# A GELU queued behind the next group's copy between PSUM banks

## The chip, the cores and the metric

The kernel runs on one core of one Trainium2 chip. The metric is the device time of one execution in microseconds (us). Below, TensorE is also PE (its weight loads PEld), VectorE is DVE, ScalarE is ACT, GpSimd is POOL and SyncE is SP, as the profile names them.

## What is computed

The program is a trunk of two decoder layers over 512 tokens of width 1024, in float32. Each layer has a mixer (attention and a short convolution in layer 0, gated linear attention in layer 1), then a gated MLP, then a per-layer embedding. The change touches the MLP alone:

```python
def _conv_ffn(h, w_up, conv_w, conv_b, w_down):
    u = _causal_depthwise_conv(h @ w_up, conv_w) + conv_b   # width 3, per column
    gate, up = jnp.split(u, 2, axis=-1)                     # 2816 columns each
    return (jax.nn.gelu(gate, approximate=False) * up) @ w_down
```

## The kernel before

Activations lie transposed: 128 features on the partitions, 512 tokens along the free dimension. Every float32 matmul is done as three passes over operands split into a high and a low part (`wh`, `wl` of weights, `uh`, `ul` of activations): ScalarE makes the high part by a copy, VectorE the low part by a subtraction (`split`, L109 and L110; `cut`, L142 and L143; `cut_blocks`, L819 and L820).

The up-projection (`ffn`) works through 11 column groups, `d` from 0 to 10. A group is 256 value columns and 256 gate columns. The value columns are two plain products (`value`, L162 to L164, 512 tokens wide), into the PSUM banks `V0` and `ps`. The gate columns use a scheme with seven half-size products instead of eight (`seven`, L872 to L874, 256 tokens wide), into the banks `W`, `V`, `X` and `Y`. Some products are summed on top of others, so the generator `seven` moves partial sums between banks by ScalarE copies, each of half a bank: L883 and L884 (W to X and Y), L890 (V to `more`), L893 (Y to X, here called the second copy) and L897 (X to Y). TensorE needs the second copy before it can go on with X's right half. To cover the copies, `seven` yields, and the loop puts pieces of the value product between: twelve matmuls 512 wide lie between the last product into Y's left half and the first product into X's right half.

While a group's products run, the weights of the next group are loaded (`loaded`, L941, one load of 1 MB for the value and one for the gate columns), cut and combined (L843, L844, L851, L854). The results of a group go through `taps`: scaling by the norm's row `R` (L923, L926, L929), then the three taps of the convolution, one on ScalarE (L930) and two on VectorE (L932). Two buffers tagged `zt` hold a group's gate half `g` and value half `y`; there are two of them, so the next group's L930 waits until they are read. Then come the GELU (L1061, ScalarE, 1024 wide), the product with the value half (`place`, L973 for the first four groups, L983 after that, VectorE), and in groups 4 to 9 `split_one(d - 4)`, which splits one of the activations kept by the first four groups (L109 and L110) for the down-projection. `split_acts` does the last two of these eight splits in the last group.

TensorE's instructions are issued in the order of the program text (`manual_schedule(engines={ET.PE})`). The other engines' orders are made when the program is built, by a scheduler that takes instructions by priority, which falls along the program text, as its own model of time finds them ready. On the chip each engine then takes its instructions in that fixed order and waits on semaphores. In the program before, the scheduler puts the GELU of group `d` behind the second copy of group `d + 1` for `d` from 0 to 4 and ahead of it for `d` from 5 to 9, and it pulls all eight splits into the time of groups 1 to 5.

Of the kernel before, what the change touches and what calls it, by code (L numbers as in the profile page):

```python
# [13 lines left out]
AF = mybir.ActivationFunctionType  # L14
# [42 lines left out]
class Kernel:  # L57
# [799 lines left out]
    def seven(self, od, ws, xg, forms, keep=True):  # L857

        nc = self.nc
        H = S // 2
        mm = nc.tensor.matmul
        W, V = self.pa(), self.pa()[:, :H]
        X, Y = self.ps(), self.ps()
        plain, t13, t2 = ws

        def product(out, w, c, x, first=False):
            kw = dict(skip_group_check=True)
            for j in range(ND // 2):  # L870
                (wh, wl), (xh, xl) = w(j, c), x(j)
                mm(out, wh, xh, start=first and j == 0, stop=False, **kw)  # L872
                mm(out, wh, xl, start=False, stop=False, **kw)  # L873
                mm(out, wl, xh, start=False, stop=j == ND // 2 - 1, **kw)  # L874

        def tokens(u, half):
            c = slice(half * H, (half + 1) * H)
            return lambda j: (xg[2 * j + u][0][:, c], xg[2 * j + u][1][:, c])

        s1, s2, s3, s4 = (lambda j, q=q: forms[j][q] for q in range(4))  # L880
        left, right = slice(0, H), slice(H, S)
        product(W[:, left], plain, 0, tokens(0, 0), True)
        nc.scalar.copy(X[:, left], W[:, left])  # L883
        nc.scalar.copy(Y[:, left], W[:, left])  # L884
        yield
        product(V, t13, 0, s1, True)
        more = V
        if keep:
            more = self.sp.tile([P, S], F32, tag="acc", name=self.nm("more"), bufs=1)[:, :H]
            nc.scalar.copy(more, V)  # L890
        product(X[:, left], plain, 1, tokens(1, 0))
        product(Y[:, left], t2, 0, s2)
        nc.scalar.copy(X[:, right], Y[:, left])  # L893
        yield
        last = self.cut_blocks(od)
        product(X[:, right], t13, 1, s3)
        nc.scalar.copy(Y[:, right], X[:, right])  # L897
        yield
        product(Y[:, left], last, 1, s4)
        product(X[:, right], last, 0, tokens(1, 1))  # L900
        yield X, Y, more

    def ffn(self, i, project, next_gain):


        nc, a, tc = self.nc, self.a, self.tc
# [5 lines left out]
        with tc.tile_pool(name=f"ffn{i}", bufs=1) as fp:  # L912
            self.mlp = fp
            kept, acts, fours = [None] * NF, [None] * NF, []
            groups = NF // 2

            def both():
                return fp.tile([P, 2, S], F32, tag="zt", name=self.nm("zt"), bufs=2)

            def taps(y, ps, f, more=None):  # L920
                z = fp.tile([P, S], F32, tag="z", name=self.nm("z"), bufs=3)
                if more is None:
                    nc.vector.tensor_tensor(z, ps, R, ALU.mult)  # L923
                else:
                    h2 = lambda x: x.rearrange("p (u t) -> p u t", u=2)
                    nc.vector.tensor_tensor(  # L926
                        h2(z), h2(ps), more.unsqueeze(1).to_broadcast([P, 2, S // 2]), ALU.add
                    )
                    nc.vector.tensor_tensor(z, z, R, ALU.mult)  # L929
                nc.scalar.activation(y, z, AF.Identity, scale=w2[:, f : f + 1], bias=bb[:, f : f + 1])  # L930
                for tap, w in ((1, w1), (2, w0)):
                    nc.vector.scalar_tensor_tensor(  # L932
                        out=y[:, tap:], in0=z[:, : S - tap], scalar=w[:, f : f + 1], in1=y[:, tap:],
                        op0=ALU.mult, op1=ALU.add,
                    )
# [11 lines left out]
            def value(w, ps, k0, k1):  # L947
                for k in range(k0, k1):
                    self.mm3(ps, w(k, 0, P), xg[k], start=k == 0, stop=k == ND - 1)

            def prepare(d):

                rv, rg = loaded(d)
                w1 = column(rv, 1)
                ev, od = self.by_parity(rg)
                ws = self.seven_forms(ev, od, rg)
                return self.seven(od, ws, xg, self.forms), w1, column(rv, 0)

            def begin(d, steps, w):

                ps = self.pa()
                value(w, ps, 0, 6)
                next(steps)
                value(w, ps, 6, ND)
                return lambda y: taps(y[:, 1], ps, NF + 2 * d + 1)

            def place(d, g, y):

                f = 2 * d
                if f < 8:  # L970
                    kept[f : f + 2] = [self.fp.tile([P, S], F32, tag=other[0], name=self.nm("u")) for _ in range(2)]
                    for u in range(2):
                        nc.vector.tensor_tensor(kept[f + u], g[:, u], y[:, u], ALU.mult)  # L973
                    return
                if d == groups - 1:
                    x = y
                else:
                    if f % 4 == 0:
                        fours.append(self.four(fp, F32))
                    x = fours[-1][:, f % 4 : f % 4 + 2]  # L980
                kept[f : f + 2] = [x[:, 0], x[:, 1]]
                pairs[f] = x
                nc.vector.tensor_tensor(x, g, y, ALU.mult)  # L983
# [3 lines left out]
            def split_one(f):  # L987

                tag = other[1 if f < 4 else 0]
                h = self.fp.tile([P, S], F32R, tag=tag, name=self.nm("uh"))  # L990
                pool, tag = (self.fp, tag) if f < 7 else (self.sp, "R")
                acts[f] = h, pool.tile([P, S], F32R, tag=tag, name=self.nm("ul"))
                self.split(acts[f], kept[f])
# [6 lines left out]
            def split_acts():  # L1000
                for f in (6, 7):
                    split_one(f)
# [32 lines left out]
            steps, w1c, w0c = ready  # L1035
            with tc.manual_schedule(engines={ET.PE}):
                late = begin(0, steps, w1c)
                for d in range(groups):
                    g, y = both(), both()
                    next(steps)  # L1040
                    V0 = self.pa()
                    value(w0c, V0, 0, ND // 2)
                    if d == 0:
                        self.end_norm()
                    next(steps)
                    value(w0c, V0, ND // 2, ND)
                    if d == 0:
                        R = self.spread()
                    X, Y, more = next(steps)
                    rest = late  # L1050

                    if d + 1 < groups:
                        steps, w1c, w0c = prepare(d + 1)
                        late = begin(d + 1, steps, w1c)
                    else:
                        split_acts()
                    rest(y)
                    taps(y[:, 0], V0, NF + 2 * d)
                    taps(g[:, 0], X, 2 * d)
                    taps(g[:, 1], Y, 2 * d + 1, more)  # L1060
                    nc.scalar.activation(g, g, AF.Gelu)  # L1061
                    place(d, g, y)
                    if 4 <= d < groups - 1:
                        split_one(d - 4)
            self.begin_norm(mine)
            finish = lambda m: self.advance(m, next_gain)
            if i == 1:
# [903 lines left out]
```

## Time and profile before

| | us |
|---|---|
| time before, median of 3 runs | 1207.76 |
| lowest and highest | 1206.56, 1208.12 |
| time of the profiled execution | 1206.43 |
| its span | 1204.7 |
| busy: PE, DVE, ACT | 1197.7, 968.3, 665.3 |
| granted TensorE clock, mean | 1.00 |
| GELUs (L1061), 22 | 23.4 busy, 1062 ns each |
| second copies and their like in the down-projections (L893), 29 | 365 ns each (median) |

The profile is of one execution. A row of a timeline gives the start and the duration in us, the engine, the line, the operation, what it writes and reads, and in brackets how long the engine sat idle before it and what ended that. A row of a stretch gives its bounds, its length, and the busy time of PE, PEld, DVE, ACT and POOL with the number of instructions, then the granted clock, the share of the DMA engines and GB/s. Ends of matmuls are modelled; their starts are recorded.

### The profile page before, as it was taken

To read this page: it belongs to the slowest core of one execution; us is meant where nothing else is said; L and a number is where in the kernel's file an instruction comes from. 1 tells how busy PE (TensorE), PEld (TensorE's weight loads), DVE (VectorE), ACT (ScalarE), POOL (GpSimd) and SP (SyncE) were. 2 spreads that over 40 slices of the span, in tenths; PEclk is the share of its full clock that TensorE was granted. 3 is DMA by queue.
4 is the path that set the end of the run, shared out by engine and by line. 5 is a ranking of instruction groups with operands and counts; after the bars stand their busy time and mean duration, and the time that the engine had idled before them with its cause. 6 is when DMAs were issued, how large, how long until landed. Compare 5 with 4: busy or idle time off the path is not lost.

```text
span 1204.7 us, 17692 instructions
## 1 busy us (share of the span) xinstructions
PE 1197.7 (99%) x7013; PEld 1036.9 (86%) x7013; DVE 968.3 (80%) x1527; ACT 665.3 (55%) x1081; POOL 43.8 (4%) x64
## 2 busy tenths in 40 slices
PE   9999999999999999999999999999999999999998
PEld 8877788999899889888988988889998899888887
DVE  6786587899998986746579876677999999988595
ACT  7466455656555644534573564555565645646374
POOL 2600000000000000000100000000000000000000
PEclk9999999999999999999999999999999999999999
DMA  7321322423333242222322222313242423322501
GB/s 222 93 85 45 96 74 70 140 71 108 103 106 104 91 137 97 96 89 94 115 93 68 73 70 71 105 49 127 70 141 70 136 75 120 134 88 97 210 1 70
DMA packets 111127, 117.61 MB, mean 98 GB/s; under 512 B 2840, under 2 KB 106322, under 8 KB 111044
## 3 DMA queue, kind: packets, MB, share of 16 engines
q1 hardware_dynamic: 109680, 115.35, 29.2%
q8 instruction: 55, 0.90, 0.3%
q0 software_dynamic: 560, 0.42, 0.3%
q10 hardware_dynamic: 804, 0.70, 0.2%
q14 instruction: 28, 0.23, 0.1%
HBM read 114.37 MB, written 2.10 MB: 97 GB/s over the span
## 4 chain that ended last, share of the span: by engine, by line
PE 87%; DVE 8%; ACT 2%; issue 1%; POOL 1%; DMA 0%; ACTq 0%; DVEq 0%; POOLq 0%
PE ps L162 12%; PE ps L163 12%; PE ps L164 12%; PE pa L163 7%; PE pa L162 7%; PE pa L164 7%; PE ps L872 5%; PE ps L874 5%; PE ps L873 5%; PE pa L872 2%; PE pa L874 2%; PE pa L873 2%; DVE wl L143 2%; PE ps L1371 1%; PE ps L1369 1%
## 5 line engine op out<-in xcount | busy, mean ns | idle before, releaser
L142 ACT ACTIVATE wh<-raw 128x1024 fp32r<-128x1024 f32 (+4 forms) x154 | 152.4, 991 | 155.1 <-PE ps L163 109.4
L143 DVE TENSOR_TENSOR wl<-raw,wh 128x1024 fp32r<-128x1024 f32 (+4 forms) x154 | 175.6, 1142 | 50.1 <-ACT wh L142 49.7
L819 ACT ACTIVATE wh<-raw 128x1024 fp32r<-128x1024 f32 x78 | 82.8, 1061 | 118.4 <-DVE raw L844 65.2
L932 DVE SCALAR_TENSOR_TENSOR zt<-z,vfa,zt 128x510 f32<-128x510 f32 (+1 forms) x176 | 130.6, 744 | 11.7 <-ACT zt L930 11.2
L820 DVE TENSOR_TENSOR wl<-raw,wh 128x1024 fp32r<-128x1024 f32 x78 | 95.3, 1222 | 19.3 <-ACT wh L819 19.2
L930 ACT ACTIVATE zt<-z,vfb 128x512 f32<-128x512 f32 x88 | 71.1, 810 | 28.9 <-DVE four L983 12.8
L162 PE MATMUL ps<-b,wh 128*128 128x512 f32 x192 | 76.8, 400 | 0.0
L163 PE MATMUL ps<-b,wh 128*128 128x512 f32 x192 | 75.1, 391 | 0.0
L164 PE MATMUL ps<-b,wl 128*128 128x512 f32 x192 | 75.0, 391 | 0.0
L163 PE MATMUL pa<-b,wh 128*128 128x512 f32 x176 | 69.0, 392 | 0.0
L163 PE MATMUL pa<-a,wh 128*128 128x512 f32 x176 | 69.0, 392 | 0.0
L162 PE MATMUL pa<-a,wh 128*128 128x512 f32 x176 | 69.0, 392 | 0.0
L162 PE MATMUL pa<-b,wh 128*128 128x512 f32 x176 | 69.0, 392 | 0.0
L164 PE MATMUL pa<-a,wl 128*128 128x512 f32 x176 | 68.4, 389 | 0.0
L164 PE MATMUL pa<-b,wl 128*128 128x512 f32 x176 | 68.4, 389 | 0.0
L872 PE MATMUL ps<-four,wh 128*128 128x256 f32 x232 | 65.1, 281 | 0.5 <-ACT ps L893 0.5
L874 PE MATMUL ps<-four,wl 128*128 128x256 f32 x232 | 64.4, 278 | 0.0
L873 PE MATMUL ps<-four,wh 128*128 128x256 f32 x232 | 64.2, 277 | 0.0
L162 PE MATMUL ps<-a,wh 128*128 128x512 f32 x160 | 63.1, 394 | 0.0
L163 PE MATMUL ps<-a,wh 128*128 128x512 f32 x160 | 62.6, 392 | 0.0
L164 PE MATMUL ps<-a,wl 128*128 128x512 f32 x160 | 62.5, 391 | 0.0
L162 PE MATMUL ps<-uh,wh 128*128 128x512 f32 x128 | 50.3, 393 | 0.0
(475 smaller groups left out, 3491.5 us busy)
## 6 DMA issues: line engine op xcount, KB each, us to landing
raw<-in_ffn_w_up_dram SPq DMA_DIRECT2D x44, 1024.0 KB, 5.0
raw<-in_ffn_w_down_dram SPq DMA_DIRECT2D x13, 1024.0 KB, 4.8
raw<-in_hy_w_in_dram SPq DMA_DIRECT2D x8, 1024.0 KB, 5.1
raw<-in_gla_w_in_dram SPq DMA_DIRECT2D x8, 1024.0 KB, 5.1
raw<-in_ffn_w_down_dram SPq DMA_DIRECT2D x8, 768.0 KB, 4.1
raw<-in_ple_w_gate_dram SPq DMA_DIRECT2D x6, 1024.0 KB, 4.8
raw<-in_hy_w_out_dram SPq DMA_DIRECT2D x16, 256.0 KB, 4.2
raw<-in_gla_w_out_dram SPq DMA_DIRECT2D x4, 1024.0 KB, 4.8
```

The lines of the kernel that those rows point to most:

```text
L142: nc.scalar.activation(hv, v, AF.Copy)
L143: nc.vector.tensor_tensor(lv, v, hv.bitcast(F32), ALU.subtract)
L162: mm(out, lh, rh, start=start, stop=False, **kw)
L163: mm(out, lh, rl, start=False, stop=False, **kw)
L164: mm(out, ll, rh, start=False, stop=stop, **kw)
L819: nc.scalar.activation(h, src, AF.Copy)
L820: nc.vector.tensor_tensor(l, src, h.bitcast(F32), ALU.subtract)
L872: mm(out, wh, xh, start=first and j == 0, stop=False, **kw)
L873: mm(out, wh, xl, start=False, stop=False, **kw)
L874: mm(out, wl, xh, start=False, stop=j == ND // 2 - 1, **kw)
L930: nc.scalar.activation(y, z, AF.Identity, scale=w2[:, f : f + 1], bias=bb[:, f : f + 1])
L932: nc.vector.scalar_tensor_tensor(out=y[:, tap:], in0=z[:, : S - tap], scalar=w[:, f : f + 1], in1=y[:, tap:], op0=ALU.mult, op1=ALU.add,)
```

## The change

`seven` keeps the instruction of the second copy in `self.copied`. In the loop, the GELU, `place` and `split_one` of a group become a function `ended`. It is called in the next turn of the loop, after the step of the generator that issues the second copy, inside `issue_after(self.copied.ins)`. That adds, for each instruction of the block on the copy's engine, which is ScalarE, an ordering edge behind the copy. So the GELU and the `uh` part of `split_one` (ScalarE) stand behind the next group's second copy in ScalarE's queue; `place` and the `ul` part (VectorE) follow them by their data and by their later place in the text. The first `next(steps)` moves ahead of `both()` in the loop. The last group's `ended` is called behind the loop, with no such edge.

```diff
         product(Y[:, left], t2, 0, s2)
-        nc.scalar.copy(X[:, right], Y[:, left])
+        self.copied = nc.scalar.copy(X[:, right], Y[:, left])
         yield
...
                 late = begin(0, steps, w1c)
+                ended = None
                 for d in range(groups):
+                    next(steps)
+                    if ended:
+                        with tc.issue_after(self.copied.ins):
+                            ended()
                     g, y = both(), both()
-                    next(steps)
                     V0 = self.pa()
                     value(w0c, V0, 0, ND // 2)
...
                     taps(g[:, 1], Y, 2 * d + 1, more)
-                    nc.scalar.activation(g, g, AF.Gelu)
-                    place(d, g, y)
-                    if 4 <= d < groups - 1:
-                        split_one(d - 4)
+
+                    def ended(d=d, g=g, y=y):
+                        nc.scalar.activation(g, g, AF.Gelu)
+                        place(d, g, y)
+                        if 4 <= d < groups - 1:
+                            split_one(d - 4)
+
+                ended()
```

## The prediction

> **What bounds the kernel now.** I read the page first, then the busy time of each engine in the stretches of the MLP up-projection, then the timelines around the copy that the change names. On the page TensorE (PE) is busy nearly the whole span.
>
> ```profile
> span 1204.7 us, 17692 instructions
> ...
> PE 1197.7 (99%) x7013; PEld 1036.9 (86%) x7013; DVE 968.3 (80%) x1527; ACT 665.3 (55%) x1081; POOL 43.8 (4%) x64
> ```
>
> That 99% is an average and its ends are modelled, so I looked at single column groups. The stretches below each run from the first value matmul behind one group's second copy to the same matmul of the next group (length first, then busy time of PE, PEld, DVE, ACT, POOL). The first five are of layer 0, the last three of layer 1.
>
> ```profile
> 213.66:234.25 20.59, 20.59 (x135) 18.63 (x133) 18.12 (x26) 12.50 (x17) 0.00 (x0) 1.00 0.32 102
> 275.42:296.01 20.59, 20.59 (x135) 18.63 (x133) 20.54 (x30) 12.03 (x20) 0.00 (x0) 1.00 0.31 103
> 296.01:316.94 20.93, 20.93 (x134) 18.65 (x133) 18.87 (x25) 12.12 (x18) 0.00 (x0) 1.00 0.30 101
> 316.94:338.06 21.12, 20.88 (x134) 18.58 (x133) 19.64 (x27) 11.95 (x17) 0.00 (x0) 1.00 0.32 101
> 379.24:399.82 20.58, 20.58 (x134) 18.62 (x133) 18.72 (x25) 11.33 (x16) 0.00 (x0) 1.00 0.31 103
> 895.29:915.88 20.59, 20.59 (x134) 18.63 (x133) 20.54 (x30) 11.90 (x20) 0.00 (x0) 1.00 0.32 103
> 915.88:936.72 20.84, 20.84 (x134) 18.66 (x133) 18.86 (x25) 12.10 (x18) 0.00 (x0) 1.00 0.31 101
> 936.72:957.82 21.10, 20.84 (x134) 18.53 (x133) 19.63 (x27) 11.91 (x17) 0.00 (x0) 1.00 0.31 101
> ```
>
> An undisturbed group takes 20.59 us, and it does so with VectorE (DVE) busy for 18.12, 18.72 or 20.54 of them. A period that does not follow VectorE's load is TensorE's own pace. Two groups in each layer are longer, and only those can be won. The Trainium skill (Perfetto Trace Analysis, Identifying the Most-Contended Engine) would judge TensorE by its weight loads, and 86% of them would leave room of some 168 us. The trace does not bear that out here: the loads are busy 18.63 us in every undisturbed group, whatever the other engines do.
>
> What makes the two groups longer is seen at the copy.
>
> ```profile
> 316.83 0.28 PE L874 MATMUL ps<-four,sq 128*128 128x256 f32 x1
> ...
> 319.46 0.39 PE L164 MATMUL pa<-a,wl 128*128 128x512 f32 x1
> 320.09 0.38 PE L872 MATMUL ps<-four,wh 128*128 128x256 f32 x1 [0.24 <-ACT ps L893]
> ...
> 316.56 1.06 ACT L819 ACTIVATE wh<-raw 128x1024 fp32r<-128x1024 f32 x1
> 318.70 1.06 ACT L1061 ACTIVATE zt<-zt 128x1024 f32<-128x1024 f32 x1 [1.08 <-DVE zt L932]
> 319.67 0.36 ACT L893 COPY ps<-ps 128x256 f32<-128x256 f32 x1
> ```
>
> The last product into Y's left half starts its last matmul at 316.83, so the copy could run when ScalarE (ACT) is done with L819, at about 317.6. But the GELU of the group before stands ahead of it, and waits 1.08 us for VectorE. The copy starts at 319.67, about 2.1 us late. TensorE has twelve value matmuls to cover that, then stands until 320.09. VectorE was late because of work that the scheduler had placed one group earlier: four splits of kept activations (L110) between 279 and 285 us, the reason for the 20.54 above.
>
> ```profile
> 279.42 1.28 DVE L110 TENSOR_TENSOR ul<-u,uh 128x512 fp32r<-128x512 f32 x2
> 281.29 0.68 DVE L110 TENSOR_TENSOR ul<-u,uh 128x512 fp32r<-128x512 f32 x1
> 284.29 0.68 DVE L110 TENSOR_TENSOR ul<-u,uh 128x512 fp32r<-128x512 f32 x1
> ```
>
> **The change, part by part.** Nothing is computed more or less: the built programs have the same instructions. In them TensorE's, SyncE's and GpSimd's orders are the same; only ScalarE's and VectorE's differ, inside the two up-projections.
>
> *The copy goes ahead of the GELU.* For five GELUs in each layer (those of groups 5 to 9) this is a swap; for groups 0 to 4 the copy was ahead already. The gain is what the two long groups hold over 20.59: (20.93 - 20.59) + (21.12 - 20.59) = 0.87 us in layer 0, and (20.84 - 20.59) + (21.10 - 20.59) = 0.76 us in layer 1, together 1.63 us. The later four swaps of a layer win nothing, since their groups take 20.59 already. The first long group, 20.93, has its copy ahead of the GELU even now; its excess should go because the cluster of splits goes (next part).
>
> *The GELU, the product behind it and the moved split wait for the copy.* What that costs is read from an undisturbed group with the old order.
>
> ```profile
> 399.71 0.28 PE L874 MATMUL ps<-four,sq 128*128 128x256 f32 x1
> 402.57 0.28 PE L872 MATMUL ps<-four,wh 128*128 128x256 f32 x1
> ...
> 398.61 1.06 ACT L819 ACTIVATE wh<-raw 128x1024 fp32r<-128x1024 f32 x1 [0.42 <-PE ps L873]
> 400.23 1.06 ACT L1061 ACTIVATE zt<-zt 128x1024 f32<-128x1024 f32 x1 [0.56 <-DVE zt L932]
> 401.19 0.37 ACT L893 COPY ps<-ps 128x256 f32<-128x256 f32 x1
> 402.58 0.82 ACT L930 ACTIVATE zt<-z,vfb 128x512 f32<-128x512 f32 x1 [1.02 <-DVE four L983]
> ...
> 401.32 1.23 DVE L983 TENSOR_TENSOR four<-zt,zt 128x1024 f32<-128x1024 f32 x1
> 403.43 1.54 DVE L932 SCALAR_TENSOR_TENSOR zt<-z,vfa,zt 128x511 f32<-128x511 f32 x2 [0.89 <-ACT zt L930]
> 405.13 1.23 DVE L143 TENSOR_TENSOR wl<-raw,wh 128x1024 fp32r<-128x1024 f32 x1 [0.16 <-ACT wh L142]
> 406.89 0.69 DVE L923 TENSOR_TENSOR z<-pa,R 128x512 f32<-128x512 f32 x1 [0.54 <-PE pa L164]
> 407.76 1.23 DVE L143 TENSOR_TENSOR wl<-raw,wh 128x1024 fp32r<-128x1024 f32 x1 [0.18 <-ACT wh L142]
> ```
>
> The copy becomes ready at 399.71 + 0.28 = 399.99 and can fill most of the 0.56 us in which ScalarE idles before the GELU. It would be out of the way by about 400.34 (0.37, less some overlap), so the GELU starts about 0.11 us later than at 400.23. What waits for that is the product L983, then L930 and L932 of the next group. Behind these VectorE idles 0.16 + 0.54 + 0.18 = 0.88 us, two of the three for work that TensorE releases. So 0.11 is absorbed, and I cost it at nothing. Without that cover it would cost 0.11 x 10 = 1.1 us, and if each GELU lost a whole copy, 0.37 x 10 = 3.7 us.
>
> *The splits (L109 on ScalarE, L110 on VectorE) move with it.* Six of a layer's eight now stand one by one behind the GELUs of groups 4 to 9, and the other two follow behind the last of these. Two L110 took 1.28 us above, so one adds some 0.6 us to VectorE in each of these groups, while groups 0 to 4 lose theirs. Its place is straight behind L983, where VectorE idles 0.89 us until L930 is done; 0.6 fits. On ScalarE the copy into `uh` fits into the 1.02 us before L930, which waits for L983 anyway. Behind the last group three splits stand together: 3 x 0.6 + 0.11 = 1.91 us against idle time of 0.89 + 0.88 = 1.77 us, so VectorE could be 0.14 us late there, 0.28 us over both layers. I take nothing for it, because it meets a weight cut for the down-projection and not a matmul, and keep 0.28 as the bound. Groups 1 to 4 only get lighter, and were at 20.59 already: no gain there.
>
> The sum is -1.63 us. The profiled execution took 1206.43 us (span 1204.7), so it would become 1204.8; the median of the runs is 1207.76, 1.33 above the profiled one, and becomes **1206.1 us**. A difference under 0.2% (2.4 us) is about what a measurement of this kernel can tell from no change, so this is a gain too small to be told for certain.
>
> **The rivals.**
>
> *More is won than the two groups.* The copies of this scheme have waiters of their own:
>
> ```profile
> L897 ACT COPY ps<-ps x29: 359/367/371, 197.8 to 1104.8; 128x256 f32<-128x256 f32 x29
> ...
>   PEld ps L872: 2.8, 8
> ```
>
> If the lighter VectorE queue also freed L897's eight waits, which lie partly in the down-projections, 2.8 us more would go: 1206.1 - 2.8 = 1203.3. For it: the cluster of splits delays whatever comes behind. Against it: the down-projections' order is unchanged.
>
> *Nothing is won.* The copy L893 goes early, but VectorE's lag lets another copy be late in the same group, and TensorE stands there instead: 1207.8. For it: the group of 20.93 us was long with its copy already ahead of the GELU. Against it: the cluster that made VectorE lag is itself gone.
>
> *The queue binds.* The GELU waits behind a copy that waits for TensorE, and the loop copy, GELU, L983, L930, L932 sets the pace. The price is the 1.1 to 3.7 us from above less 1.63: 1207.2 to 1209.8. It decides where the GELU slips by more than the 0.88 us of idle time; the rows make it 0.11. The Trainium skill (Perfetto Trace Analysis, Tensor Engine Instruction) says that ScalarE and VectorE are strict FIFOs, which is the rule against this change; the trace agrees in the rows at 318.70 and 319.67, where a ready copy stood behind a waiting GELU.
>
> *Slower: a weight cut holds the copy L897.* Without the splits the scheduler puts the cut L142 ahead of L897 in two more groups of each layer (1 and 3). L142 needs a load that has just landed. One group has this order already:
>
> ```profile
> 259.69 1.05 ACT L142 ACTIVATE wh<-raw 128x1024 fp32r<-128x1024 f32 x1
> 260.64 0.36 ACT L897 COPY ps<-ps 128x256 f32<-128x256 f32 x1
> ...
> 261.71 0.28 PE L872 MATMUL ps<-four,wh 128*128 128x256 f32 x1
> ...
> raw<-in_ffn_w_up_dram SPq DMA_DIRECT2D x44, 1024.0 KB, 5.0
> ```
>
> Here L897 ends at 261.00, 0.71 us before TensorE needs it. If ScalarE reaches the cut 2 us before its load (these take 5.0 us), TensorE stands 2.0 - 0.71 = 1.3 us in two groups of two layers, 5.2 us; less 1.63 that is +3.6: 1211.3. It decides from a load that is 0.71 us late. Against it: this group lost nothing, and the copy does not wait here.
>
> **How the numbers follow.** Forecast 0.54; more is won 0.15; nothing is won 0.13; the queue binds 0.07; a cut holds the copy 0.11. The forecast lies 0.8 us inside the 2.4 us line and the three runs spread over 1.6 us, so 0.04 of its 0.54 counts as faster. Faster: 0.15 + 0.04 = 0.19. Within 0.2%: 0.50 + 0.13 + 0.07 = 0.70. Slower: 0.11. The range goes from 1203.5, near the far end of the second case, to 1209.8, the upper price of the binding queue; it leaves out the slower case and some of the scatter.
>
> **What would show it.** Right: all ten stretches of each layer at 20.59 us; L893 ahead of L1061 everywhere and starting within 0.1 us of its last matmul or of L819's end; no waiter at L893; L110 one by one behind L983, with L932's idle of 0.89 shrunk to about 0.3. Wrong: a stretch over 20.7 us after the change; waits of TensorE on L897 or L883 in the up-projections; ScalarE's L142 waiting for a load ahead of L897; or GELUs that start later than 0.3 us behind VectorE's last L932.

## The result, and the profile after

The changed kernel takes 1205.18 us (median of 22 runs, 1204.47 to 1206.30) against 1207.15 us of the kernel before (22 runs, 1206.05 to 1208.16): 1.97 us less, a ratio of 0.9985 with a 95% interval of 0.9978 to 0.9991. That is a small gain, most of whose interval lies within the 0.2% that the prediction named. The profiled execution took 1205.84 us.

In the kernel after, lines up to 1030 keep their numbers, the GELU is L1067 and the residual add of the down-projection is L1189 (before: L1061 and L1181). The head of its page:

```profile
span 1204.1 us, 17688 instructions
...
PE 1196.2 (99%) x7013; PEld 1036.6 (86%) x7013; DVE 969.2 (80%) x1527; ACT 667.2 (55%) x1081; POOL 43.9 (4%) x64
```

Next the same stretches as in the prediction: from the first value matmul behind one group's second copy to that of the next group. Length, then busy time of PE, PEld, DVE, ACT, POOL. The first three are of layer 0, the last two of layer 1.

```profile
297.00:317.59 20.59, 20.59 (x134) 18.62 (x133) 19.50 (x26) 11.95 (x17) 0.00 (x0) 1.00 0.33 104
317.59:338.18 20.59, 20.59 (x135) 18.63 (x133) 19.33 (x26) 11.85 (x17) 0.00 (x0) 1.00 0.31 103
...
379.35:399.94 20.59, 20.59 (x135) 18.63 (x133) 19.34 (x26) 11.85 (x17) 0.00 (x0) 1.00 0.32 104
916.06:936.64 20.58, 20.58 (x134) 18.62 (x133) 19.65 (x27) 11.94 (x17) 0.00 (x0) 1.00 0.32 104
936.64:957.23 20.59, 20.59 (x135) 18.63 (x133) 19.34 (x26) 11.86 (x17) 0.00 (x0) 1.00 0.31 103
```

The four long stretches (20.93, 21.12, 20.84, 21.10) are gone. From the start of group 0's stretch to that of the last group's it is now 399.94 - 193.18 = 206.76 us in layer 0; before it was 399.82 - 192.18 = 207.64. In layer 1 it is 1018.99 - 812.23 = 206.76, before 1019.58 - 812.05 = 207.53. These are 0.88 and 0.77, the two terms of the sum. The spans differ by only 0.6, because in this one execution the work ahead of layer 0's groups took 1.0 us longer (193.18 against 192.18; in the traces of all kernels here it takes 192.0 to 193.6). ScalarE at the place where the copy had come 2.1 us late:

```profile
317.79 0.36 ACT L893 COPY ps<-ps 128x256 f32<-128x256 f32 x1 [0.35 <-PE ps L874]
318.06 1.06 ACT L1067 ACTIVATE zt<-zt 128x1024 f32<-128x1024 f32 x1
```

The copy now waits for TensorE and not for VectorE, and the GELU behind it waits for nothing. Of the 11 executions of `e4_down_pinned` below, one took 2004.04 us at a granted clock of 0.556; it is in the median but not in the ratio.

### The profile page after: what moved, and what is told of

It reads as the page before. It is cut to its first block, busy times and chain, and to the rows that moved or that the text cites. A ratio compares the mean times of both kernels' runs of the same rounds, so it can differ in the third digit from the quotient of the medians.

```text
span 1204.1 us, 17688 instructions
## 1 busy us (share of the span) xinstructions
PE 1196.2 (99%) x7013; PEld 1036.6 (86%) x7013; DVE 969.2 (80%) x1527; ACT 667.2 (55%) x1081; POOL 43.9 (4%) x64
## 4 chain that ended last, share of the span: by engine, by line
PE 88%; DVE 6%; issue 2%; ACT 2%; POOL 1%; DMA 0%; DVEq 0%; POOLq 0%; ACTq 0%
PE ps L162 12%; PE ps L163 12%; PE ps L164 12%; PE pa L163 7%; PE pa L162 7%; PE pa L164 7%; PE ps L872 6%; PE ps L874 6%; PE ps L873 5%; PE pa L872 2%; PE pa L874 2%; PE pa L873 2%; DVE wl L143 1%; PE ps L1379 1%; PE ps L1377 1%
## 5 line engine op out<-in xcount | busy, mean ns | idle before, releaser
L142 ACT ACTIVATE wh<-raw 128x1024 fp32r<-128x1024 f32 (+4 forms) x154 | 152.5, 992 | 156.8 <-PE ps L163 109.2
L143 DVE TENSOR_TENSOR wl<-raw,wh 128x1024 fp32r<-128x1024 f32 (+4 forms) x154 | 175.6, 1141 | 51.1 <-ACT wh L142 50.1
L819 ACT ACTIVATE wh<-raw 128x1024 fp32r<-128x1024 f32 x78 | 82.8, 1062 | 120.8 <-DVE raw L844 65.1
L932 DVE SCALAR_TENSOR_TENSOR zt<-z,vfa,zt 128x510 f32<-128x510 f32 (+1 forms) x176 | 130.7, 745 | 5.3 <-ACT zt L930 4.7
L930 ACT ACTIVATE zt<-z,vfb 128x512 f32<-128x512 f32 x88 | 71.1, 810 | 20.8 <-DVE four L983 8.3
L164 PE MATMUL ps<-b,wl 128*128 128x512 f32 x192 | 75.0, 391 | 0.0
L164 PE MATMUL pa<-a,wl 128*128 128x512 f32 x176 | 68.4, 389 | 0.0
L164 PE MATMUL pa<-b,wl 128*128 128x512 f32 x176 | 68.4, 389 | 0.0
L872 PE MATMUL ps<-four,wh 128*128 128x256 f32 x232 | 64.7, 279 | 0.0
L873 PE MATMUL ps<-four,wh 128*128 128x256 f32 x232 | 64.2, 277 | 0.0
L164 PE MATMUL ps<-a,wl 128*128 128x512 f32 x160 | 62.5, 391 | 0.0
```

Of the source, the lines that this page charges most:

```text
L142: nc.scalar.activation(hv, v, AF.Copy)
L143: nc.vector.tensor_tensor(lv, v, hv.bitcast(F32), ALU.subtract)
L164: mm(out, ll, rh, start=False, stop=stop, **kw)
L819: nc.scalar.activation(h, src, AF.Copy)
L932: nc.vector.scalar_tensor_tensor(out=y[:, tap:], in0=z[:, : S - tap], scalar=w[:, f : f + 1], in1=y[:, tap:], op0=ALU.mult, op1=ALU.add,)
```

## The experiments

A word on reading them: the medians of these kernels lie within 2 us of each other, at about the edge of what timing tells apart, but the undisturbed stretches of one trace repeat to 0.01 us, and group 0's stretch is 21.48 in every trace. So the verdicts rest on the stretches. Each trace is of one execution, though, and in layer 0 of two of them the work already starts later in group 0 than in all others; that is said there. Each label is the name of a kernel. A ratio in brackets is to the kernel before, with its interval.

**The two halves of the change, each alone.** First the order of GELU and copy without moving the splits (`e1_copy_first`):

```
                     with tc.issue_after(self.copied.ins): ended()    # ended(): GELU, place
...
+                    if 4 <= d < groups - 1: split_one(d - 4)         # at its old place in the text
```

> The order alone: the copy L893 goes ahead of the GELU as in the changed kernel, while the eight splits of a layer (L109, L110) keep their early, clustered places in groups 1 to 5. Cluster theory (VectorE's lag from the clustered splits is the cause, and the old order only hands it on to TensorE): the first long group of each layer stays long, 20.93 us in layer 0 and 20.84 in layer 1, because its copy was ahead already and the four splits still stand in the group before it; the second falls from 21.12 and 21.10 to 20.59, since nobody waits at L893 any more. That is 0.53 + 0.51 = 1.04 us less than before, 0.59 more than the changed kernel. Order theory (the place of the GELU is the whole cause): all stretches 20.59, 1.63 less than before, the same as the changed kernel. Third case: VectorE's lag meets another copy, and the second group stays over 20.8.

Then the splits alone (`e2_splits_pinned`): GELU and product at their old place, and only the split waits for the next group's copy.

```
+                    nc.scalar.activation(g, g, AF.Gelu)
+                    place(d, g, y)
                     def ended(d=d):
                         if 4 <= d < groups - 1: split_one(d - 4)
```

> The splits alone: GELU and product keep their old place ahead of the next group's copy L893, and only the splits wait for that copy, one in each of groups 5 to 9. Cluster theory: VectorE is never more than its usual 0.5 us late for the GELU, the copy ends about 1.2 us after it is ready, the twelve value matmuls cover that, and all stretches are 20.59: 1.63 us less than before, the same as the changed kernel. Order theory: the GELU still stands ahead of the copy in groups 5 to 9, TensorE waits at L893 there, and at least one group of each layer stays over 21.0, so no more than 0.59 less than before.

`e1_copy_first` took 1206.36 us (ratio 0.9993, 0.9984 to 1.0002), `e2_splits_pinned` 1205.58 (0.9989, 0.9981 to 0.9998). The stretches of the first, with the heavy group ahead of the long one:

```profile
275.25:295.84 20.59, 20.59 (x135) 18.63 (x133) 20.54 (x30) 12.02 (x20) 0.00 (x0) 1.00 0.32 103
295.84:316.70 20.86, 20.86 (x135) 18.70 (x133) 18.94 (x25) 12.16 (x18) 0.00 (x0) 1.00 0.31 101
316.70:337.29 20.59, 20.59 (x135) 18.63 (x133) 18.76 (x25) 11.32 (x17) 0.00 (x0) 1.00 0.31 103
```

and of the second, that of the group that was the first long one:

```profile
297.00:317.59 20.59, 20.59 (x135) 18.63 (x133) 19.45 (x26) 11.91 (x17) 0.00 (x0) 1.00 0.31 103
```

The order alone cures the second long group and leaves 0.27 us in the first (0.20 in layer 1, at 20.79). The splits alone cure both, although GELU and copy stand in the old order: all groups behind group 0 take 20.59 in both layers. So the order theory falls. Moving the splits is enough by itself; moving the GELU gives 1.16 of the 1.63 us. What is left in `e1_copy_first` has two places on ScalarE:

```profile
300.64 0.82 ACT L930 ACTIVATE zt<-z,vfb 128x512 f32<-128x512 f32 x1 [1.29 <-DVE four L983]
301.36 1.04 ACT L142 ACTIVATE wh<-raw 128x1024 fp32r<-128x1024 f32 x1
302.31 0.36 ACT L897 COPY ps<-ps 128x256 f32<-128x256 f32 x1
...
312.86 0.63 ACT L819 ACTIVATE sq<-raw 128x512 fp32r<-128x512 f32 x1 [1.85 <-DVE raw L851]
313.39 0.37 ACT L883 COPY ps<-pa 128x256 f32<-128x256 f32 x1
```

Two other copies between banks, L897 and L883, each stand behind an operation that waits for VectorE (L897 behind L142, which stands behind L930). The Trainium skill (Perfetto Trace Analysis, Tensor Engine Instruction) says that ScalarE and VectorE work their queues strictly in order, and these rows agree: L883 starts 313.39 - 295.84 = 17.55 us into its group, where it could have started at 15.30, as a row of `c6_six` below shows (352.58 - 337.28). The first matmul behind L897 starts 6.87 us into an undisturbed group (261.71 - 254.84, from the prediction's rows), which is 302.71 here. L897 ends at 302.67, and TensorE loses time all the same. The weight loads show why, first of the undisturbed group of the kernel before, then of this one:

```profile
261.49 0.19 PEld L872 LDWEIGHTS ps<-four,wh 128*128 128x128 f32 x1
...
302.73 0.19 PEld L872 LDWEIGHTS ps<-four,wh 128*128 128x128 f32 x1 [0.28 <-ACT ps L897]
```

What waits for the copy is already the load of that matmul's weights. It usually starts 0.22 us ahead of the matmul, at 6.65 us into the group (261.49 - 254.84), here 302.49, so L897 ends 0.18 too late. By the starts of the matmuls 0.15 us of the group's 0.27 go at L897 and 0.12 at L883; in layer 1 it is 0.15 and 0.05.

**Doses of the cluster.** Up to here I took the cluster for the cause, with a capacity: what exceeds VectorE's spare time costs. Three kernels test that with the changed kernel's order, by putting more splits behind one GELU.

```
-                        if 4 <= d < groups - 1:
-                            split_one(d - 4)
+                        if d == 6:                      # c6_six; c2_pairs: two behind 4, 6, 8; c3_threes: three behind 5, 8
+                            for f in range(6): split_one(f)
```

> Dose of the cluster, with the copy ahead of the GELU everywhere: two splits behind each of the GELUs of groups 4 and 6, and four together behind that of group 8. A group without a split holds VectorE for 18.1 to 18.7 us of 20.59, so it has some 1.9 us to spare, and a split (L110) costs it 0.62. Capacity theory (a cluster costs what it exceeds the spare time by): two cost 1.24 and fit, all stretches of groups 4 to 8 stay 20.59; four cost 2.48, 0.6 over, and a stretch behind group 8 is longer by 0.2 to 0.6 us, as in the kernel with the early cluster of four (0.27 and 0.20). Rival (only what stands before the GELU counts, and the new order takes up any cluster): 20.59 everywhere.

> The same with three splits behind the GELU of group 5 and five together behind that of group 8. Capacity theory: three cost 1.86 us, just the spare time, so 20.59 or less than 0.1 more; five cost 3.1, 1.2 over, and the stretches behind group 8 are longer by 0.6 to 1.2 us in sum. Rival: 20.59 everywhere.

> The same with all six splits behind the GELU of group 6, to which the scheduler adds a seventh and, one group later, the eighth. Capacity theory: seven cost 4.3 us, 2.5 over the spare time of one group and 0.6 over that of two, so TensorE stands in the next two stretches for 1.2 to 2.5 us in sum per layer: 2.4 to 5.0 us more than the changed kernel, about 1208 to 1210. Rival (the order takes up the cluster): 20.59 everywhere, no difference from the changed kernel.

They took 1205.05, 1205.29 and 1205.14 us (ratios 0.9985, 0.9987 and 0.9987, the last with an interval of 0.9978 to 0.9996). Every stretch behind group 0 is 20.59, in all three, for doses of two, three, four, five and seven. My capacity theory falls. The heaviest group of `c6_six` and the next one:

```profile
337.28:357.86 20.58, 20.58 (x134) 18.62 (x133) 20.45 (x29) 14.27 (x23) 0.00 (x0) 1.00 0.30 101
357.86:378.45 20.59, 20.59 (x134) 18.63 (x133) 19.99 (x28) 12.44 (x19) 0.00 (x0) 1.00 0.31 103
```

VectorE's load, 20.45 and 19.99 us, is in sum no lighter than in `e1_copy_first` (20.54 and 18.94). ScalarE shows the difference:

```profile
352.58 0.36 ACT L883 COPY ps<-pa 128x256 f32<-128x256 f32 x1 [1.69 <-PE pa L874]
...
353.45 0.63 ACT L819 ACTIVATE sq<-raw 128x512 fp32r<-128x512 f32 x1 [0.23 <-DVE raw L851]
...
358.06 0.36 ACT L893 COPY ps<-ps 128x256 f32<-128x256 f32 x1
...
361.37 1.06 ACT L1067 ACTIVATE zt<-zt 128x1024 f32<-128x1024 f32 x1
...
363.28 0.36 ACT L897 COPY ps<-ps 128x256 f32<-128x256 f32 x1
363.72 0.82 ACT L930 ACTIVATE zt<-z,vfb 128x512 f32<-128x512 f32 x1
```

The GELU starts 361.37 - 357.86 = 3.5 us into its group, later than in the long groups of before (318.70 - 316.94 = 1.8 in the second, 2.4 in the first) and in that of `e1_copy_first` (2.4), and TensorE loses nothing. But here L893 stands ahead of the GELU, L883 ahead of `sq`, and L897 ahead of L930. So the next theory: VectorE's lag costs TensorE time only through a copy that stands behind an operation waiting for VectorE.

**The copies put ahead, the cluster left.** One place at a time, first L883, in the kernel with the order alone and in the kernel before (`e6_banks_first`, `e7_before_banks`; in these two L883 is L887, L893 is L901, L897 is L905 and L930 is L938):

```
-        return plain, self.cut_blocks(ev), self.more_forms(ev, od)
...
-        nc.scalar.copy(Y[:, left], W[:, left])
+        spread = nc.scalar.copy(Y[:, left], W[:, left])      # L884 of before
...
+            with self.tc.issue_after(spread.ins):
...
+                    t2 = self.cut_blocks(t2[0], False)       # the cut into sq
```

> The kernel with the order alone (copy L893 ahead of the GELU, early cluster of four splits), and in it the small cut into `sq` (L819, 128x512), which waits for VectorE's L851, queued behind the copies L883 and L884 and no longer ahead of them. Nothing else of ScalarE's order changes, and the cluster stays. Queue theory (VectorE's lag costs TensorE time only where a copy between banks stands on ScalarE behind an operation that waits for VectorE; there were two such places in the long group, L883 behind `sq`, which ran 2.2 us late, and L897 behind L930 and L142): the wait at L883 goes, that at L897 (0.11) stays: 20.86 becomes 20.70 to 20.77 in layer 0, and 20.79 becomes 20.70 in layer 1; all other stretches 20.59. Cluster theory (the load itself costs the time, wherever the copies stand): 20.86 and 20.79 stay, or the time comes back in the next stretch.

> The same edit, `sq` behind L883 and L884, in the kernel before, with its GELU ahead of the copy L893 and its early cluster. Queue theory: the wait at L883 goes from the first long group, 20.93 becomes 20.70 in layer 0 and 20.84 about 20.73 in layer 1. But the copy of the second long group still stands behind the GELU, whose start VectorE sets, so TensorE, now 0.2 us earlier, waits there 0.2 us longer: 21.12 becomes about 21.3 and 21.10 about 21.2, and the sum over both groups stays (42.05 and 41.94): nothing is won. Rival (the stalls are independent terms, as the prediction's sum took them): the second groups keep 21.12 and 21.10, and 0.23 + 0.11 = 0.34 us are won in all.

They took 1206.55 us (0.9995, 0.9986 to 1.0005) and 1207.41 us (1.0007, 0.9997 to 1.0016). TensorE no longer waits at L883 in either. In `e6_banks_first` the long stretch of layer 1 fell from 20.79 to 20.73, but that of layer 0 went from 20.86 to 20.89, which the expectation missed. There L897 ended 0.17 us later into its group. But that is not shown to be a stall handed on: in layer 0 a cut L819 of group 0 already starts 7.49 us into its stretch and not 7.31 as in `e1_copy_first`, and the GELUs behind it come 0.15 to 0.2 us later, up to the long group. The stretches of `e7_before_banks` (the pair of long groups of layer 0, then that of layer 1):

```profile
296.74:317.75 21.01, 20.89 (x135) 18.58 (x133) 19.12 (x26) 12.78 (x18) 0.00 (x0) 1.00 0.31 101
317.75:338.88 21.13, 20.83 (x135) 18.53 (x133) 19.32 (x26) 11.53 (x17) 0.00 (x0) 1.00 0.31 100
916.70:937.42 20.72, 20.72 (x135) 18.59 (x133) 18.82 (x25) 12.71 (x18) 0.00 (x0) 1.00 0.31 102
937.42:958.56 21.14, 20.84 (x134) 18.53 (x133) 19.31 (x26) 11.40 (x17) 0.00 (x0) 1.00 0.31 100
```

The pairs sum to 42.14 and 41.86; before they were 42.05 and 41.94. Layer 0 does not compare like with like here either. ScalarE's cut in its group 0:

```profile
200.15 1.06 ACT L819 ACTIVATE wh<-raw 128x1024 fp32r<-128x1024 f32 x1 [1.82 <-DMA raw<-in_ffn_w_up_dram]
```

It waits for a weight load and starts 200.15 - 192.33 = 7.82 us into its stretch, before 199.49 - 192.18 = 7.31, and the GELUs of the next groups come about 0.5 us later than before (that in the stretch of group 3 at 4.42 us, before 3.88). All layers of the other kernels, and layer 1 of these two, have this cut at 7.31; whether it is late by chance or by the edit, no run here shows. In layer 1, which starts as before, the first stretch is 0.12 us shorter and the second 0.04 longer: TensorE, less late, does wait longer at L893, but gives back 0.04 of the 0.12 and not all of it. So neither expectation is borne out in full. "Nothing is won" is not shown, and the 0.08 us that are left are little to build on in one execution. That a stall need not be handed on whole is plain from `e1_copy_first`, where the place of L893 alone gave all that the second stretches held, 0.53 and 0.51 us, and nothing came back behind them.

In layer 0 of this kernel a new stall came besides, in group 3, whose stretch took 21.16:

```profile
260.95 1.06 ACT L142 ACTIVATE wh<-raw 128x1024 fp32r<-128x1024 f32 x1 [0.49 <-DMA raw<-in_ffn_w_up_dram]
261.92 0.37 ACT L905 COPY ps<-ps 128x256 f32<-128x256 f32 x1
```

A weight cut waited for its load ahead of the copy. TensorE's matmul usually starts at 254.99 + 6.87 = 261.86 and the load of its weights 0.22 earlier, but the copy ended at 262.29. That is the prediction's slower rival, in one place, and in the layer that was late from group 0 on.

The last kernel of this kind, `e8_turned_first`, goes back to `e1_copy_first` and queues each L930 behind its group's L897 (L930 is L931 here, L932 L933, and the GELU L1071):

```
+        self.turned = nc.scalar.copy(Y[:, right], X[:, right])
...
+                with tc.issue_after(self.turned.ins):
                     nc.scalar.activation(y, z, AF.Identity, ...)
```

> The kernel with the order alone (copy L893 ahead of the GELU, splits in their early places), and in it each L930, which waits for VectorE, queued behind the copy L897 of its group and no longer ahead of it; with that the scheduler's order of the later groups has the copies L883 and L884 ahead of `sq` as well. The cluster stays: the same four splits stand behind the GELU of the same group. Queue theory (VectorE's lag costs TensorE time only through a copy between banks that stands behind an operation waiting for VectorE): the first long group falls from 20.86 and 20.79 to 20.59 although VectorE stays about 2 us late for the GELU in it, all stretches are 20.59, and the time is that of the changed kernel, 0.5 us below the kernel with the order alone. Load theory (a cluster of four splits costs what it costs): 20.8 to 20.9 stays in that group or comes in the next.

It took 1205.86 us (0.9988, 0.9979 to 0.9997). The stretch behind its heavy group (which took 20.60), and ScalarE in it:

```profile
296.27:316.86 20.59, 20.59 (x135) 18.63 (x133) 19.24 (x26) 11.64 (x17) 0.00 (x0) 1.00 0.31 103
```

```profile
298.13 1.06 ACT L1071 ACTIVATE zt<-zt 128x1024 f32<-128x1024 f32 x1 [1.08 <-DVE zt L933]
...
302.13 0.37 ACT L897 COPY ps<-ps 128x256 f32<-128x256 f32 x1
302.43 0.81 ACT L931 ACTIVATE zt<-z,vfb 128x512 f32<-128x512 f32 x1
```

The GELU is 1.9 us into its group, and all groups behind group 0 take 20.59 or 20.60. This kernel alone would not settle it. Behind the same cluster the GELU of `e1_copy_first` came 2.4 us into its long group, and in the group behind that one, at 1.7 us (318.44 - 316.70), TensorE lost nothing although L897 and L883 stood behind the same operations. So 1.9 us may be too little lag to tell the orders apart. What tells them apart is `c6_six`, with 3.5 us of lag and the copies ahead, against `e1_copy_first`, with 2.4 us and the copies behind. With `e2_splits_pinned` this makes two separate cures: take away VectorE's lag, or take the copies out from behind what waits for it.

**A large dose of the queue** (`e3_gelu_behind_turned`):

```
-                        with tc.issue_after(self.copied.ins): ended()
-                    g, y = both(), both()
...
                     next(steps)
...
+                        with tc.issue_after(self.turned.ins): ended()
+                    g, y = both(), both()
```

> A large dose of the queue: GELU, product and split are held behind the third copy (L897) of the next group and not its second (L893); in the changed kernel L897 follows L893 by 5.0 us, so the GELU slips by about 4.9 us and not by 0.06. The rival 'the queue binds' (copy, GELU, L983, L930, L932 set the pace; it decides from a slip of 0.88 us of VectorE's idle time) gives up to 4.9 - 0.88 = 4.0 us in each of the ten groups of a layer: 80 us over both. Phase theory: no matmul waits for the GELU within its group, the slip shifts GELU, L983, L930 and L932 as a block against TensorE once, at the start, and costs again only at the end of each layer's groups: under 5 us a layer, and stretches of 20.59 as long as the value of the next group has a bank to go to. Between the two: L930 and L932 come late for L923, the banks of V0 come free late, and some of the stretches are longer.

It took 1215.85 us (1.0071, 1.0058 to 1.0085). One of its stretches of layer 0, and the GELU in it:

```profile
378.57:399.16 20.59, 20.59 (x134) 18.63 (x133) 18.95 (x26) 11.78 (x17) 0.00 (x0) 1.00 0.31 103
```

```profile
384.40 1.05 ACT L1067 ACTIVATE zt<-zt 128x1024 f32<-128x1024 f32 x1
```

The GELU starts 5.8 us into its group, against 0.47 in the changed kernel, and every stretch of layer 0 behind group 0 is still 20.59. In layer 1 only the last two are longer, 20.86 and 21.49; why there and not in layer 0 is not shown. The rest of the price, 3.4 us in layer 0 and 4.2 in layer 1, falls behind the groups, where the down-projection meets the operands late:

```profile
449.26 0.38 PE L872 MATMUL pa<-a,wh 128*128 128x256 f32 x1 [1.25 <-ACT a L109]
```

So the phase theory held, with the end dearer than "under 5 us a layer" only in layer 1 (1.2 + 4.2 = 5.4).

**The same remedy elsewhere.** In the changed kernel TensorE's waits on L897 are in the down-projections, three in each layer, where the cut L142 stands ahead of the copy. `e4_down_pinned` holds the cut back in every block unit, `e5_third_pinned` only in the third:

```
+        self.turned = nc.scalar.copy(Y[:, right], X[:, right])
...
-                    pump(1)
+                    with tc.issue_after(self.turned.ins):    # e5_third_pinned: only if s == 2
+                        pump(1)
```

> The same remedy for the stalls that the changed kernel still has: in the down-projections ScalarE's weight cut L142 (0.96 us) stands ahead of the copy L897, which is ready about 0.1 us after the cut has begun, and TensorE stands at L897 three times in each layer: 0.24 + 0.25 + 0.24 us in layer 0 and 0.24 + 0.19 + 0.21 in layer 1, restarts included. Here the first weight cuts behind L897 are queued after that copy. Queue theory: the three stalls of each layer go, 1.37 us less than the changed kernel. Rival: the cut is then 0.4 us later, VectorE's L143 and the weight loads behind it are later, and as much or more comes back as waits for weights: 0 to +1.4 us.

> Of the three weight cuts per layer that the down-projection variant held behind L897, only the last. In that variant the first pin moved its 0.24 us to a wait of the next matmul for the residual add L1189 (0.48, before 0.13), and the second to L820 (0.34 plus a restart), while nothing came back behind the third in layer 0. Theory (each pin is a trade by itself; the third is free): the third stall goes in both layers, 0.24 + 0.21 = 0.45 us less than the changed kernel, the two others stay as they are. Rival (the delay of the third cut comes back as the waits of the projection behind the layer, L285 and others, which were 0.3 to 0.4 us longer there): nothing in layer 0's sum changes or layer 1 loses 0.4, in all 0 to 0.2 more than the changed kernel.

`e4_down_pinned` took 1205.60 us (0.9987, 0.9978 to 0.9996), no less than the changed kernel. All six waits on L897 are gone, and others stand in their place. From the last group's stretch to the end of the projection behind it, its trace takes 401.40 us in layer 0, against 401.34 in the changed kernel, and 145.92 against 145.17 in layer 1, so 0.8 us more in sum. VectorE and TensorE behind the first unit of layer 0:

```profile
454.32 1.23 DVE L143 TENSOR_TENSOR wl<-raw,wh 128x1024 fp32r<-128x1024 f32 x1
...
457.27 0.68 DVE L1189 TENSOR_TENSOR xT<-xT,ps 128x512 f32<-128x512 f32 x1
```

```profile
457.30 0.39 PE L164 MATMUL ps<-uh,wl 128*128 128x512 f32 x1
458.01 0.50 PE L162 MATMUL ps<-uh,wh 128*128 128x512 f32 x1 [0.32 <-DVE xT L1189]
```

L143, which needs the cut, pushes the residual add L1189 back: it starts 457.27 - 399.43 = 57.84 us behind the start of the last group's stretch, in the changed kernel 57.71 (457.65 - 399.94). TensorE, now earlier, needs the bank that this add reads. `e5_third_pinned` took 1204.71 us (0.9982, 0.9973 to 0.9991), the shortest median of all kernels here, though not told apart from the changed kernel's by timing. TensorE at the third unit there:

```profile
484.71 0.39 PE L164 MATMUL ps<-uh,wl 128*128 128x512 f32 x1
484.93 0.28 PE L872 MATMUL ps<-a,wh 128*128 128x256 f32 x1
485.05 0.28 PE L873 MATMUL ps<-a,wh 128*128 128x256 f32 x1
```

and in the changed kernel:

```profile
485.38 0.39 PE L164 MATMUL ps<-uh,wl 128*128 128x512 f32 x1
485.74 0.39 PE L872 MATMUL ps<-a,wh 128*128 128x256 f32 x1
485.96 0.28 PE L873 MATMUL ps<-a,wh 128*128 128x256 f32 x1
```

From L164 to L873 it is 0.34 us instead of 0.58, the forecast 0.24. In layer 1 the part from the last group's stretch to the end of the projection behind it fell from 145.17 to 144.96, the forecast 0.21, and nothing came back. In layer 0 that part fell from 401.34 to 400.98, by more than the stall; where the other 0.12 went is not shown.

## Why the prediction was right, and where it was not

*What bounds the kernel.* Right: 20.59 us is TensorE's own pace. It stayed with VectorE busy for 18.8 to 20.5 us of a group (`e1_copy_first`), and with a GELU 5.8 us into its group (`e3_gelu_behind_turned`). The sentence "all ten stretches of each layer at 20.59" was wrong in one of ten: group 0's stretch is 21.48 before and after, and no term of the sum.

*The gain.* Right in size: 0.88 and 0.77 measured, 0.87 and 0.76 forecast. The reason given for the first long group, that its excess goes because the cluster of splits goes, was confirmed by the pair of halves. The step that failed is the sentence "What makes the two groups longer is seen at the copy". It holds for the second long group alone. In the first, TensorE lost nothing at L893. By the starts of its matmuls it lost 0.09 us at L897 and 0.25 at L883 in layer 0, and 0.13 and 0.12 in layer 1. ScalarE there, in the kernel before:

```profile
302.45 0.36 ACT L897 COPY ps<-ps 128x256 f32<-128x256 f32 x1
...
313.12 0.64 ACT L819 ACTIVATE sq<-raw 128x512 fp32r<-128x512 f32 x1 [1.85 <-DVE raw L851]
313.66 0.37 ACT L883 COPY ps<-pa 128x256 f32<-128x256 f32 x1
```

So L893 was one of three copies that pass VectorE's lag on. The cluster of splits that made VectorE late stands one group ahead of the first long group, but two ahead of the rows at 318.70, and not "one group earlier". That the four excesses were added as if none depended on another did no harm, because the lag and the copy's place were both cured at once. Whether one of them alone would have paid in full depends on which: the second group's did in `e1_copy_first`, and of the 0.12 us by which `e7_before_banks` shortened the first one in layer 1, 0.04 came back in the second.

*The GELU's slip.* Forecast 0.11 us, measured 0.06: the GELU starts 0.47 us into the group that the prediction had chosen, and not 0.41.

```profile
400.41 1.07 ACT L1067 ACTIVATE zt<-zt 128x1024 f32<-128x1024 f32 x1
```

It cost nothing, as forecast, but not for the reason given. The 0.88 us of VectorE's idle time were no threshold: in `e3_gelu_behind_turned` a slip of 5.4 us left the groups of layer 0 as they were. A GELU that comes later shifted the work behind it once. It cost where something waited for that work, mostly in the down-projection.

*The splits.* VectorE's load with one split is 19.34 in the stretch that had 18.72 without, so 0.62 each, as forecast. L932 waits 0.28 us where it had 0.89, forecast "about 0.3":

```profile
362.44 1.54 DVE L932 SCALAR_TENSOR_TENSOR zt<-z,vfa,zt 128x511 f32<-128x511 f32 x2 [0.28 <-ACT zt L930]
```

The three splits behind the last group came nearest to harm. The third `uh` copy waited for VectorE ahead of L142 and L897:

```profile
404.16 0.63 ACT L109 ACTIVATE uh<-u 128x512 fp32r<-128x512 f32 x1 [0.58 <-DVE ul L110]
...
405.65 0.36 ACT L897 COPY ps<-ps 128x256 f32<-128x256 f32 x1
```

L897 ends at 406.01. TensorE's matmul starts at 399.94 + 6.87 = 406.81 and the load of its weights 0.22 us earlier, so some 0.6 us were to spare. Of the prediction's bound for this place, 0.28 us over both layers, hardly anything is seen behind the group: that part took 401.34 us against 401.29 before in layer 0, and 145.17 against 145.18 in layer 1.

*The time.* Forecast 1206.1, measured 1205.18. Of the 0.9 us between them, 0.61 is the starting point: the median of before is 1207.15 over 22 runs, not 1207.76 over three. The forecast 1.63 us from there give 1205.5, inside the interval of 1204.5 to 1206.1 that the ratio leaves. The stretches are the better test of the sum: 1.65 us there against 1.63.

*The rivals.* "More is won" looked to L897's waits; in the up-projections they did go, in the down-projections they stayed, and the two variants there show that 0.45 us of them can be won and that the rest moves to other waits. "Nothing is won" did not happen, but its mechanism is real: in `e1_copy_first` TensorE loses time at two other copies, with L893 ahead of the GELU. "The queue binds" was wrong in its point of decision, as told. "A weight cut holds the copy" did not happen in the changed kernel, but did in group 3 of `e7_before_banks`. (By the stretches, the two groups in which the change puts L142 ahead of L897 are 2 and 4, and not 1 and 3 as the prediction counts.) The copy's start there lies 1.1 us later in the group than in the row that the prediction showed (261.92 - 254.99 against 260.64 - 254.84). The margin of 0.71 us was taken to the matmul; to the load of its weights it was 0.49. That leaves 0.6, and the stretch is 0.57 longer than 20.59.

## What to carry to other kernels

When TensorE waits at a copy, look one engine further: ask what stands ahead of the copy in its queue, and which engine that waits for. Several such stalls in neighbouring groups may come from one lag, and removing one of them can hand a part on to the next; remove the lag, or take all the copies out from behind it. Judge how late a copy is by the weight load that waits for it, not by the matmul. Pinning one instruction behind another is a trade at each place by itself: of three equal pins in the down-projection one gave 0.24 us and two moved the wait elsewhere.

## What was not expected of the hardware

A missed start costs more than the delay of the matmul itself. In the last rows above from the changed kernel, L872 begins 0.36 us behind L164 and not 0.22, takes 0.39 and not 0.28, and the next matmul follows it after 0.22 and not 0.12. So some 0.1 us goes behind the wait, after the operand is there. About the same 0.1 stood behind the other stalls at these copies, also in `e1_copy_first`, where the copy had ended 0.04 us ahead of the matmul's usual start. The rows of weight loads above show where it may go. Without a stall the load of L872 (261.49) runs under the matmul ahead and is over before its own begins (261.71). Behind the copy it starts together with its own matmul (both at 302.73), so its 0.19 us no longer lie under other work. That the 0.1 us is a part of this load is a reading of these rows; no experiment here separates it.
